# A fused two-layer encoder on one core: the order of the opening stage (warm-up, first loads, scaling of x)

## The chip, the cores and the metric

The kernel runs on one core of one Trainium2 chip. The metric is the time on the device in microseconds (us), from start to end of one execution. Each engine of the core (TensorE, VectorE, ScalarE, GpSimd, SyncE) runs its own list of instructions; semaphores tie them together. In the rows, PE is TensorE's matrix product, PEld its weight load, DVE is VectorE, ACT is ScalarE, POOL is GpSimd and SP is SyncE, which here only issues loads.

## What is computed

x has 512 rows of 1024, mem has 256 rows of 1024, all in fp32. Two layers follow each other, an mLSTM layer and a latent-attention layer, each with attention to the memory. Cut to what matters for the opening:

```python
mem_n = rmsnorm(mem, mem_norm)
mk, mv = split_cols(mem_n @ w_kv, [MEM_WIDTH, MEM_WIDTH])   # memory keys and values, 256 x 512 each
mk = rmsnorm(mk.reshape(bsz, nm, MEM_HEADS, MEM_HEAD_DIM), k_gain)
h = rmsnorm(x, norm_g)                                      # first layer
... = split_cols(h @ w_in, [2 * M_WIDTH, M_WIDTH, M_WIDTH, M_WIDTH, M_HEADS, M_HEADS, MEM_WIDTH, MEM_WIDTH])
```

## The kernel before

Every matrix product is done with operands split into a high part and a low part (`split`: ScalarE writes the high part, VectorE the rest), as three products: high with high, low with high (line 157) and high with low (line 162). Weights come in chunks of 128 x 1024 numbers, 512 KB. `load` (lines 137 to 147) makes the high part "wh" (line 130) and the low part "wl" (line 131) of a chunk; there are two buffers of each.

The opening stage goes up to the first products with x, at about 50 us:

- Line 120 and 121: twenty transpositions of the identity on TensorE, which need only the identity.
- Lines 411 to 413: ScalarE's queue issues the loads of the parameter columns pv (first its first 8 columns, then the rest) and of the positions. The first 8 columns scale the memory (line 133 and 134 in `load_memT`). Lines 481 to 483 multiply columns of the rest on VectorE.
- Lines 488 to 496, 533 to 541: SyncE's queue issues everything else, in this order: the transposed memory's first two pieces, each followed by a half of the first weight chunk, more of the memory with chunks 2 to 4, x in four loads with chunk 5 between them, chunks 6 to 8, the memory by rows for its norm, and then, as buffers come free, the weights of the later products.
- `mem_kv` (lines 244 to 282) is a generator: the memory keys are chunks 1 to 4, the values chunks 5 to 8, each chunk being one turn (one yield), with two row tiles of memory as two accumulators "acc". After the fourth chunk the keys are copied out (line 259), squared head by head (line 187, into "tiny" and "junk" buffers), and scaled on GpSimd (lines 263, 264 and 269). After the eighth, the values are copied out and split, and the keys are transposed (line 280) into two PSUM buffers "tp" and split.
- `x_prep` (lines 503 to 530) is a generator too. It sums the squares of x (lines 187 and 511), takes the power on GpSimd (lines 182 and 183), scales the eight half tiles of x (lines 520 and 522) and ends its first turn. Then, for each of eight groups of 128 columns, four transpositions go into a "tp" buffer (line 527) and a `split` makes that group of hT (hTh and hTl, the transposed, normed x). It yields after every second group.
- `mem_norm` (lines 232 to 242) sums squares of the memory's rows on ScalarE (into "tiny" and "junk" buffers) and takes the power on GpSimd.
- At the end: three turns of `mem_kv`, one of `x_prep`, `mem_norm`, and then `weave`, which gives `x_prep` one turn after each turn of `mem_kv` and lets it finish when `mem_kv` has ended.
- After that `mem_proj` begins: its first group has 264 columns (gates and half of a query projection), three chunks of 3, 3 and 2 groups of hT, with four accumulators "acc", which are all that there are. Its second group has 256 columns and needs the same four.

This program order is not yet the order of the engines' lists. A planner goes through the program with estimated times and puts on each engine the instruction that is ready, earlier ones in the program first. Tiles with one name share a number of buffers ("tp" two, "junk" one, "tiny" forty), and a new tile has to wait until a buffer of its name is free. Only the last stage of the kernel has TensorE's order written out by hand.

Of the kernel before, what the change touches and what calls it, by code (L numbers as in the profile page):

```python
# [12 lines left out]
AF = mybir.ActivationFunctionType  # L13
ALU = mybir.AluOpType
AX = mybir.AxisListType

P = 128
S = 512
NT = 4
# [40 lines left out]
def trunk(ctx: ExitStack, tc: tile.TileContext, pv_d, pos_d, x_d, mem_d, memT_d, wmem_d, wg_d, wa_d, woa_d,  # L60
          wkva_d, wql_d, wb_d, wkvb_d, wqup_d, wob_d, out_d):
    nc = tc.nc
    V, A, G, PE = nc.vector, nc.scalar, nc.gpsimd, nc.tensor
# [11 lines left out]
    def nm(s):  # L75
        cnt[0] += 1
        return f"{s}_{cnt[0]}"
# [3 lines left out]
    def st(shape, tag, bufs=1, dt=F32):  # L81
        return POOLS.get(tag, sp).tile(shape, dt, tag=tag, bufs=bufs, name=nm(tag))
# [6 lines left out]
    def tiny(shape, dt=F32):  # L89
        return st(shape, "tiny", 40, dt)  # L90

    def s2(shape=(P, 512)):
        return st(list(shape), "s2", NS2)

    def acc(shape=(P, 512)):
        return pp.tile(list(shape), F32, tag="acc", bufs=4, name=nm("acc"))
# [4 lines left out]
    def tps(shape=(P, 512)):  # L101
        return pp.tile(list(shape), F32, tag="tp", bufs=2, name=nm("tp"))
# [14 lines left out]
    warm = cp.tile([P, 1], F32, name="warm")  # L117
    A.activation(warm, one, AF.Exp)
    wps = tps([P, P])
    for _ in range(20):  # L120
        PE.transpose(wps, ident, ident)  # L121

    def col(name, i=0):
        o = _PV[name] + i
        return pv[:, o:o + 1]
# [11 lines left out]
    def load(src, nk, ncol, pieces=1, raw=None):  # L137
        n = nk * ncol
        if raw is None:
            raw = wp.tile([P, 1024], F32, tag="wr", bufs=2, name=nm("wr"))  # L140
            nc.sync.dma_start(raw[:, :n], src)
        hi = wp.tile([P, 1024], F32R, tag="wh", bufs=2, name=nm("wh"))
        lo = wp.tile([P, 1024], F32R, tag="wl", bufs=2, name=nm("wl"))
        for i in range(pieces):
            ps_ = slice(i * n // pieces, (i + 1) * n // pieces)
            split(hi[:, ps_], lo[:, ps_], raw[:, ps_])
        return (hi[:, :n].rearrange("p (k c) -> p k c", k=nk), lo[:, :n].rearrange("p (k c) -> p k c", k=nk))

    def prod(items, start, stop):

        left = {}
        for it in items:
            left[id(it[0])] = left.get(id(it[0]), 0) + 1
        seen = set()
        for ps, a_, w_, lhs in items:
            for x in a_:
                PE.matmul(ps, x if lhs else w_[0], w_[0] if lhs else x,  # L157
                          start=start and id(ps) not in seen, stop=False)
                seen.add(id(ps))
        for ps, a_, w_, lhs in items:  # L160
            left[id(ps)] -= 1
            PE.matmul(ps, a_[0] if lhs else w_[1], w_[1] if lhs else a_[0], start=False,  # L162
                      stop=stop and left[id(ps)] == 0)

    def prod_tok(pss, act, w, nk, k0, first, last, done=None):

        n = len(pss)
        step = 1 if last else 2
        for t0 in range(0, n, step):
            prod([(pss[t], act(k0 + k, t), w[k] if isinstance(w, list) else sub(w, slice(None), k), True)  # L170
                  for t in range(t0, min(n, t0 + step)) for k in range(nk)], first, last)
            if last and done:
                done(t0, pss[t0])
            if step == 2 or t0 % 2 == 1:
                yield

    def sub(pair, *idx):
        return (pair[0][idx], pair[1][idx])

    def rpow(out, ss, mul, add, n):  # L180
        t = tiny([P, n])
        G.tensor_scalar(t, ss, mul, add, op0=ALU.mult, op1=ALU.add)  # L182
        G.tensor_tensor(out=out, in0=t, in1=mhalf[:, :n], op=ALU.pow)

    def sqsum(src, accum, scale=1.0):
        j = st([P, 512], "junk", 1, BF16)
        A.activation(j[:, :src.shape[-1]], src, AF.Square, scale=scale, accum_out=accum)  # L187
# [20 lines left out]
    def mem_raw():  # L208
        return [st([P, 2, NM], "s2", NS2) for _ in range(4)]
# [34 lines left out]
    def mem_kv(l, mT, mkT, mv, preload=None):  # L244
        for half in range(2):
            pss = [acc(), acc()]
            for c in range(4):
                i = half * 4 + c
                raw = preload[i] if preload else None
                w = raw if isinstance(raw, tuple) else load(wmem_d[l, i], 2, 512, raw=raw)  # L250
                yield from prod_tok(pss, mT, w, 2, 2 * c, c == 0, c == 3)
            if half == 0:
                ss = tiny([P, 2, 4])
                r = tiny([P, 2, 4])
                mks = []
                for t in range(2):
                    mk = s2()
                    mks.append(mk)
                    A.activation(mk, pss[t], AF.Copy)
                    for h in range(4):  # L260
                        sqsum(mk[:, h * P:(h + 1) * P], ss[:, t, h:h + 1])
                for t in range(2):
                    G.tensor_scalar(ss[:, t], ss[:, t], 1.0 / P, vs_mem[:, t:t + 1], op0=ALU.mult, op1=ALU.add)
                G.tensor_tensor(out=r.rearrange("p a b -> p (a b)"), in0=ss.rearrange("p a b -> p (a b)"),
                                in1=mhalf[:, :8], op=ALU.pow)
                for t in range(2):
                    for h in range(4):
                        hs = slice(h * P, (h + 1) * P)
                        G.tensor_scalar(mks[t][:, hs], mks[t][:, hs], r[:, t, h:h + 1], None, op0=ALU.mult)
            else:  # L270
                for t in range(2):
                    src = pss[t]
                    if preload:
                        src = s2()
                        A.activation(src, pss[t], AF.Copy)
                    split(mv[0][:, t], mv[1][:, t], src, rs_mem[:, t:t + 1])
                for t in range(2):
                    tp = tps([P, 4, P])
                    for h in range(4):
                        PE.transpose(tp[:, h], mks[t][:, h * P:(h + 1) * P], ident)  # L280
                    ts_ = slice(t * P, (t + 1) * P)
                    split(mkT[0][:, :, ts_], mkT[1][:, :, ts_], tp, gg[:, l:l + 1])
# [125 lines left out]
                                    c == 0, c == 5, lambda t, ps: done(half, t, ps))  # L408


    A.dma_start(pv[:, 0:8], pv_d[:, 0:8])
    A.dma_start(pv[:, 8:], pv_d[:, 8:])
    A.dma_start(pos, pos_d)
    tabs = cp.tile([P, 4, NT, 64], F32, name="tabs")
# [66 lines left out]
    V.tensor_tensor(out=gg[:, 0:2], in0=pv[:, _PV["mqg"]:_PV["mqg"] + 2],  # L481
                    in1=pv[:, _PV["mkg"]:_PV["mkg"] + 2], op=ALU.mult)
    V.tensor_tensor(out=gg[:, 2:3], in0=col("qgn"), in1=col("kgn"), op=ALU.mult)
    wraw = st([P, 6, 1024], "yTh"), st([P, 6, 1024], "yTl")
    pre = [wraw[0][:, i] for i in range(6)] + [wraw[1][:, i] for i in range(2)]

    mraw = mem_raw()
    for k in range(2):
        nc.sync.dma_start(mraw[0][:, k], memT_d[:, k])
        nc.sync.dma_start(pre[0][:, k * 512:(k + 1) * 512], wmem_d[0, 0][:, k * 512:(k + 1) * 512])  # L490
    for q in range(1, 4):
        nc.sync.dma_start(mraw[q], memT_d[:, q * 2:q * 2 + 2])
        if q == 1:
# [3 lines left out]
    mT = load_memT(mraw)  # L497
# [6 lines left out]
    def x_prep(xs, hT):  # L504
        rs = tiny([P, NT])
        sa = tiny([P, 2, NT])
        for half in range(2):
            for t in range(NT):
                if t % 2:
                    j = st([P, 512], "m4", 1, BF16)  # L510
                    V.scalar_tensor_tensor(out=j, in0=xs[half][t], scalar=1.0, in1=xs[half][t], op0=ALU.mult,
                                           op1=ALU.mult, accum_out=sa[:, half, t:t + 1])
                else:
                    sqsum(xs[half][t], sa[:, half, t:t + 1])
        V.tensor_tensor(out=sa[:, 0], in0=sa[:, 0], in1=sa[:, 1], op=ALU.add)
        rpow(rs, sa[:, 0], 1.0 / D, EPS, NT)
        for half in range(2):
            for t in range(NT):
                if half and t % 2:
                    A.activation(xs[half][t], xs[half][t], AF.Copy, scale=rs[:, t:t + 1])  # L520
                else:
                    V.tensor_scalar(xs[half][t], xs[half][t], rs[:, t:t + 1], None, op0=ALU.mult)
        yield
        for k in range(KT):
            tp = tps()
            for t in range(NT):
                PE.transpose(tp[:, t * P:(t + 1) * P], xs[k // 4][t][:, (k % 4) * P:(k % 4 + 1) * P], ident)
            split(hT[0][:, k], hT[1][:, k], tp, col("an", k))
            if k % 2:
                yield  # L530
# [5 lines left out]
    xs = load_x(x_d, nc.sync, wraw[1][:, 2:6].rearrange("p a (b c) -> p a b c", b=2), rest)  # L536
# [244 lines left out]
    mT = load_memT()  # L781
# [388 lines left out]
```

## Time and profile before

| | us |
|---|---|
| median of 3 runs | 771.48 |
| lowest and highest | 770.83, 771.83 |
| profiled execution | 771.22 |
| its span, first to last instruction | 769.4 |

The profile is of one execution. In its rows, times are us from the start of the span, and for a row of several instructions the time is from the first one's start to the last one's end. Behind an arrow in brackets stands the idle time of the engine just before the row, and what ended it. Matrix products overlap each other, so a group's time is more than the sum of their starts' distances by the length of the last one.

### The profile page before, as it was taken

Reading aid. Unit: us, or ns where it says so; the run is one execution under the profiler, and the core shown is the slowest. Engines: PE = TensorE matmul, PEld = TensorE weight load, DVE = VectorE, ACT = ScalarE, POOL = GpSimd, SP = SyncE. Lnnn points to the kernel's source line nnn. Section 1 sums busy time; section 2 is a strip of 40 time slices with the busy share of each in tenths; the row PEclk is TensorE's granted clock in tenths of the full one; section 3 lists DMA queues with packets and bytes.
Section 4 is the critical chain, followed back from the end, with each engine's and each line's share of the span. In section 5 each row is a group of like instructions: output and inputs, shape, how many; then the busy total and the mean of one; then the engine's idle time right before and its main releaser. Section 6 shows DMA issues by size and latency. Waiting matters only on the chain.

```text
span 769.4 us, 10978 instructions
## 1 busy us (share of the span) xinstructions
PE 756.1 (98%) x3948; PEld 648.8 (84%) x3948; DVE 486.8 (63%) x985; ACT 409.9 (53%) x958; POOL 133.2 (17%) x259
## 2 busy tenths in 40 slices
PE   9999998999999999999999999999999999999998
PEld 7798887888888888888888878999888888888886
DVE  6743699547778737765434664476778787775422
ACT  6964566345456426546333757367766665644220
POOL 0131010010110101001002131020855351700000
PEclk9999999999999999999999999999999999999999
DMA  9522120322131232225434532221322111511141
GB/s 327 202 89 104 63 79 25 109 90 101 60 107 57 86 106 83 83 83 185 144 137 155 173 110 72 69 67 58 95 75 59 56 59 36 184 55 55 65 155 55
DMA packets 25910, 76.40 MB, mean 99 GB/s; under 512 B 3072, under 2 KB 3968, under 8 KB 25856
## 3 DMA queue, kind: packets, MB, share of 16 engines
q1 hardware_dynamic: 24144, 73.44, 28.7%
q10 hardware_dynamic: 1584, 2.25, 0.8%
q8 instruction: 31, 0.51, 0.3%
q14 instruction: 23, 0.19, 0.1%
q0 software_dynamic: 128, 0.01, 0.0%
HBM read 71.49 MB, written 4.19 MB: 98 GB/s over the span
## 4 chain that ended last, share of the span: by engine, by line
PE 89%; DVE 7%; ACT 2%; POOL 1%; issue 1%; POOLq 0%; DVEq 0%; ACTq 0%
PE acc L157 49%; PE acc L162 24%; PE att L157 3%; PE att L1026 2%; PE att L162 2%; PE tp L1013 1%; PE tp L949 1%; DVE kl L629 1%; DVE tiny L328 1%; DVE wl L131 1%; PE att L715 1%; PE att L716 1%; PE att L714 1%; PE tp L121 1%; PE tp L368 1%
## 5 line engine op out<-in xcount | busy, mean ns | idle before, releaser
L131 DVE TENSOR_TENSOR wl<-wr,wh 128x1024 fp32r<-128x1024 f32 (+5 forms) x117 | 136.8, 1170 | 154.5 <-ACT wh L130 130.0
L130 ACT ACTIVATE wh<-wr 128x1024 fp32r<-128x1024 f32 (+5 forms) x117 | 117.6, 1009 | 134.5 <-PE acc L157 123.3
L157 PE MATMUL acc<-wh,hTl 128*128 128x512 f32 (+3 forms) x320 | 113.3, 366 | 0.0
L157 PE MATMUL acc<-wh,hTh 128*128 128x512 f32 (+3 forms) x320 | 112.4, 368 | 0.3 <-ACT hTh L133 0.3
L157 PE MATMUL acc<-hTh,wh 128*128 128x512 f32 x256 | 101.8, 398 | 0.0
L157 PE MATMUL acc<-hTl,wh 128*128 128x512 f32 x256 | 100.3, 392 | 0.0
L157 PE MATMUL acc<-wh,yTh 128*128 128x512 f32 (+1 forms) x224 | 84.7, 382 | 0.0
L157 PE MATMUL acc<-wh,yTl 128*128 128x512 f32 (+1 forms) x224 | 84.5, 379 | 0.0
L162 PE MATMUL acc<-wl,hTh 128*128 128x512 f32 (+3 forms) x320 | 82.0, 364 | 0.0
L162 PE MATMUL acc<-hTh,wl 128*128 128x512 f32 x256 | 69.6, 391 | 0.0
L157 PEld LDWEIGHTS acc<-wh,hTh 128*128 128x128 f32 x320 | 59.1, 188 | 9.4 <-ACT hTh L133 0.6
L157 PEld LDWEIGHTS acc<-wh,hTl 128*128 128x128 f32 x320 | 59.6, 188 | 8.7 <-DVE hTl L134 0.2
L162 PEld LDWEIGHTS acc<-wl,hTh 128*128 128x128 f32 x320 | 56.5, 188 | 8.6
L162 PE MATMUL acc<-wl,yTh 128*128 128x512 f32 (+1 forms) x224 | 60.1, 378 | 0.0
L157 PEld LDWEIGHTS acc<-hTh,wh 128*128 128x128 f32 x256 | 48.1, 188 | 9.4 <-ACT wh L130 0.3
L162 PEld LDWEIGHTS acc<-hTh,wl 128*128 128x128 f32 x256 | 47.7, 188 | 9.7
L157 PEld LDWEIGHTS acc<-hTl,wh 128*128 128x128 f32 x256 | 48.2, 188 | 9.0
L182 POOL TENSOR_SCALAR tiny<-tiny 128x2 f32<-128x2 f32 (+4 forms) x33 | 8.5, 257 | 236.2 <-ACT junk L187 68.6
L157 PEld LDWEIGHTS acc<-wh,yTh 128*128 128x128 f32 x224 | 42.1, 188 | 7.2
L157 PEld LDWEIGHTS acc<-wh,yTl 128*128 128x128 f32 x224 | 42.1, 188 | 7.1
L162 PEld LDWEIGHTS acc<-wl,yTh 128*128 128x128 f32 x224 | 41.2, 188 | 7.5
L157 PE MATMUL acc<-wh,u 128*128 128x384 f32 (+1 forms) x160 | 38.6, 364 | 1.2 <-ACT u L133 0.7
(285 smaller groups left out, 1418.5 us busy)
## 6 DMA issues: line engine op xcount, KB each, us to landing
wr<-in_wa_dram SPq DMA_DIRECT2D x46, 512.0 KB, 3.2
wr<-in_wb_dram SPq DMA_DIRECT2D x16, 512.0 KB, 3.5
wr<-in_woa_dram SPq DMA_DIRECT2D x12, 512.0 KB, 3.2
wr<-in_wob_dram SPq DMA_DIRECT2D x12, 512.0 KB, 3.2
wr<-in_wmem_dram SPq DMA_DIRECT2D x8, 512.0 KB, 3.5
yTh<-in_wmem_dram SPq DMA_DIRECT2D x5, 512.0 KB, 7.2
yTl<-in_x_dram SPq DMA_DIRECT2D x4, 512.0 KB, 8.7
u<-in_x_dram SPq DMA_DIRECT2D x4, 512.0 KB, 6.1
```

Source lines behind the costliest of these rows:

```text
L121: PE.transpose(wps, ident, ident)
L130: A.activation(hi, src, AF.Copy)
L131: V.tensor_tensor(out=lo, in0=src, in1=hi.bitcast(F32), op=ALU.subtract)
L157: PE.matmul(ps, x if lhs else w_[0], w_[0] if lhs else x, start=start and id(ps) not in seen, stop=False)
L162: PE.matmul(ps, a_[0] if lhs else w_[1], w_[1] if lhs else a_[0], start=False, stop=stop and left[id(ps)] == 0)
L182: G.tensor_scalar(t, ss, mul, add, op0=ALU.mult, op1=ALU.add)
L328: V.tensor_reduce(mx[:, j:j + 1], ps, axis=AX.X, op=ALU.max)
L368: PE.transpose(tp[:, t * P:(t + 1) * P], prs[h][t][:, kt * P:(kt + 1) * P], ident)
L629: V.scalar_tensor_tensor(out=u[:, d:], in0=raw[:, :S - d], scalar=col("cw", (3 - d) * 16 + j), in1=u[:, d:], op0=ALU.mult, op1=ALU.add)
L714: PE.matmul(ps[:, :258], ph[:, blk(c, i)], v[0][:, c], start=c == 0, stop=False)
L715: PE.matmul(ps[:, :258], low(c, i), v[0][:, c], start=False, stop=False)
L1026: PE.matmul(ps[:, i * P:(i + 1) * P], vt[:, c, h * P:(h + 1) * P], pTs[h][:, o:o + P], start=c == 0, stop=c == i)
```

## The change

Four things in the opening stage. Fifteen transpositions of the identity in place of twenty. The first half of the first weight chunk is loaded from ScalarE's queue, between the two loads of pv, and its second half goes ahead of the memory's second piece on SyncE's. The products of the first chunk are ordered so that those with its first half come first, for both row tiles. And x is scaled in two halves, each ahead of the four groups that use it and each ended by a yield, with tiles 1 and 3 of each half on ScalarE and 0 and 2 on VectorE.

```diff
--- before.py
+++ after.py
@@ -117,7 +117,7 @@
     warm = cp.tile([P, 1], F32, name="warm")
     A.activation(warm, one, AF.Exp)
     wps = tps([P, P])
-    for _ in range(20):
+    for _ in range(15):
         PE.transpose(wps, ident, ident)
 
     def col(name, i=0):
@@ -162,13 +162,14 @@
             PE.matmul(ps, a_[0] if lhs else w_[1], w_[1] if lhs else a_[0], start=False,
                       stop=stop and left[id(ps)] == 0)
 
-    def prod_tok(pss, act, w, nk, k0, first, last, done=None):
+    def prod_tok(pss, act, w, nk, k0, first, last, done=None, halves=False):
 
         n = len(pss)
         step = 1 if last else 2
         for t0 in range(0, n, step):
-            prod([(pss[t], act(k0 + k, t), w[k] if isinstance(w, list) else sub(w, slice(None), k), True)
-                  for t in range(t0, min(n, t0 + step)) for k in range(nk)], first, last)
+            its = [(pss[t], act(k0 + k, t), sub(w, slice(None), k), True)
+                   for t in range(t0, min(n, t0 + step)) for k in range(nk)]
+            prod(its[::2] + its[1::2] if halves else its, first, last)
             if last and done:
                 done(t0, pss[t0])
             if step == 2 or t0 % 2 == 1:
@@ -248,7 +249,7 @@
                 i = half * 4 + c
                 raw = preload[i] if preload else None
                 w = raw if isinstance(raw, tuple) else load(wmem_d[l, i], 2, 512, raw=raw)
-                yield from prod_tok(pss, mT, w, 2, 2 * c, c == 0, c == 3)
+                yield from prod_tok(pss, mT, w, 2, 2 * c, c == 0, c == 3, halves=preload is not None and i == 0)
             if half == 0:
                 ss = tiny([P, 2, 4])
                 r = tiny([P, 2, 4])
@@ -408,7 +409,9 @@
                                     c == 0, c == 5, lambda t, ps: done(half, t, ps))
 
 
+    wraw = st([P, 6, 1024], "yTh"), st([P, 6, 1024], "yTl")
     A.dma_start(pv[:, 0:8], pv_d[:, 0:8])
+    A.dma_start(wraw[0][:, 0, 0:512], wmem_d[0, 0][:, 0:512])
     A.dma_start(pv[:, 8:], pv_d[:, 8:])
     A.dma_start(pos, pos_d)
     tabs = cp.tile([P, 4, NT, 64], F32, name="tabs")
@@ -481,13 +484,12 @@
     V.tensor_tensor(out=gg[:, 0:2], in0=pv[:, _PV["mqg"]:_PV["mqg"] + 2],
                     in1=pv[:, _PV["mkg"]:_PV["mkg"] + 2], op=ALU.mult)
     V.tensor_tensor(out=gg[:, 2:3], in0=col("qgn"), in1=col("kgn"), op=ALU.mult)
-    wraw = st([P, 6, 1024], "yTh"), st([P, 6, 1024], "yTl")
     pre = [wraw[0][:, i] for i in range(6)] + [wraw[1][:, i] for i in range(2)]
 
     mraw = mem_raw()
-    for k in range(2):
-        nc.sync.dma_start(mraw[0][:, k], memT_d[:, k])
-        nc.sync.dma_start(pre[0][:, k * 512:(k + 1) * 512], wmem_d[0, 0][:, k * 512:(k + 1) * 512])
+    nc.sync.dma_start(mraw[0][:, 0], memT_d[:, 0])
+    nc.sync.dma_start(pre[0][:, 512:1024], wmem_d[0, 0][:, 512:1024])
+    nc.sync.dma_start(mraw[0][:, 1], memT_d[:, 1])
     for q in range(1, 4):
         nc.sync.dma_start(mraw[q], memT_d[:, q * 2:q * 2 + 2])
         if q == 1:
@@ -514,14 +516,15 @@
                     sqsum(xs[half][t], sa[:, half, t:t + 1])
         V.tensor_tensor(out=sa[:, 0], in0=sa[:, 0], in1=sa[:, 1], op=ALU.add)
         rpow(rs, sa[:, 0], 1.0 / D, EPS, NT)
-        for half in range(2):
-            for t in range(NT):
-                if half and t % 2:
-                    A.activation(xs[half][t], xs[half][t], AF.Copy, scale=rs[:, t:t + 1])
-                else:
-                    V.tensor_scalar(xs[half][t], xs[half][t], rs[:, t:t + 1], None, op0=ALU.mult)
         yield
         for k in range(KT):
+            if k % 4 == 0:
+                for t in range(NT):
+                    if t % 2:
+                        A.activation(xs[k // 4][t], xs[k // 4][t], AF.Copy, scale=rs[:, t:t + 1])
+                    else:
+                        V.tensor_scalar(xs[k // 4][t], xs[k // 4][t], rs[:, t:t + 1], None, op0=ALU.mult)
+                yield
             tp = tps()
             for t in range(NT):
                 PE.transpose(tp[:, t * P:(t + 1) * P], xs[k // 4][t][:, (k % 4) * P:(k % 4 + 1) * P], ident)
```

## Rows read from the trace of the kernel before

**Rows 1.** The page, part 1: busy us, share of the span, instructions, by engine

```profile
PE 756.1 (98%) x3948; PEld 648.8 (84%) x3948; DVE 486.8 (63%) x985; ACT 409.9 (53%) x958; POOL 133.2 (17%) x259
```

**Rows 2.** Stretches: busy us by engine, granted clock, DMA share, GB/s

```profile
5.00:7.25 2.25, 2.25 (x10) 2.06 (x9) 1.48 (x4) 1.10 (x3) 0.00 (x0) 1.00 0.82 252
7.25:20.00 12.75, 12.72 (x54) 9.94 (x54) 10.19 (x19) 10.07 (x20) 0.00 (x0) 1.00 1.04 413
22.18:38.80 16.62, 15.35 (x98) 13.54 (x97) 12.81 (x19) 15.92 (x40) 1.85 (x5) 1.00 0.42 159
```

**Rows 3.** Timeline of TensorE, opening: start, length, line, out<-in, count

```profile
1.81 4.53 PE L121 MATMUL tp<-ident 128*128 128x128 f32 x20 [1.81 <-POOL ident masks.py:199]
5.99 2.99 PE L157 MATMUL acc<-wh,qk 128*128 128x512 f32 x8
...
15.62 1.98 PE L157 MATMUL acc<-wh,qk 128*128 128x512 f32 x8
```

**Rows 4.** Timeline of ScalarE, VectorE and weight loads: first waits for loads

```profile
3.64 0.51 ACT L133 ACTIVATE qk<-s,pv 128x256 fp32r<-128x256 f32 x1 [0.98 <-DMA pv<-in_pv_dram]
...
8.99 1.15 ACT L130 ACTIVATE wh<-yTh 128x512 fp32r<-128x512 f32 x2 [0.48 <-DMA yTh<-in_wmem_dram]
...
9.68 1.69 PEld L157 LDWEIGHTS acc<-wh,qk 128*128 128x128 f32 x8 [0.21 <-ACT wh L130]
...
4.62 0.16 DVE L481 TENSOR_TENSOR gg<-pv 128x2 f32<-128x2 f32 x1 [3.23 <-DMA pv<-in_pv_dram]
```

**Rows 5.** Timeline: the scaling of x, on GpSimd, ScalarE and VectorE

```profile
21.10 1.04 POOL L183 TENSOR_TENSOR tiny<-tiny,mhalf 128x4 f32<-128x4 f32 x1
...
22.18 1.34 ACT L520 ACTIVATE yTl<-yTl,tiny 128x512 f32<-128x512 f32 x2 [0.66 <-POOL tiny L183]
...
22.18 2.46 DVE L522 TENSOR_SCALAR yTl<-yTl,tiny 128x512 f32<-128x512 f32 x6 [1.45 <-POOL tiny L183]
24.56 1.21 DVE L131 TENSOR_TENSOR wl<-yTh,wh 128x1024 fp32r<-128x1024 f32 x1
```

**Rows 6.** Timeline of TensorE in that place

```profile
21.57 2.12 PE L157 MATMUL acc<-wh,qk 128*128 128x512 f32 x8 [0.35 <-ACT wh L130]
23.52 1.04 PE L527 MATMUL tp<-ident,yTl 128*128 128x128 f32 x8
25.83 1.19 PE L162 MATMUL acc<-wl,qk 128*128 128x512 f32 x4 [1.27 <-DVE wl L131]
```

**Rows 7.** Timeline: the memory keys copied out, and squares (u: mem_norm's, s: keys')

```profile
18.09 1.09 ACT L259 ACTIVATE s<-acc 128x512 f32<-128x512 f32 x2 [0.36 <-PE acc L162]
...
25.64 0.63 ACT L187 ACTIVATE junk<-u 128x512 bf16<-128x512 f32 x1
...
30.43 0.45 POOL L239 TENSOR_TENSOR tiny<-tiny 128x2 f32<-128x2 f32 x1 [8.29 <-ACT junk L187]
...
30.83 0.30 ACT L187 ACTIVATE junk<-s 128x128 bf16<-128x128 f32 x1
```

**Rows 8.** Timeline of GpSimd: the memory keys' power and scaling

```profile
39.03 0.27 POOL L263 TENSOR_SCALAR tiny<-tiny,vs_mem 128x4 f32<-128x4 f32 x1 [5.33 <-ACT junk L187]
39.38 1.66 POOL L264 TENSOR_TENSOR tiny<-tiny,mhalf 128x8 f32<-128x8 f32 x1
41.14 5.42 POOL L269 TENSOR_SCALAR s<-s,tiny 128x128 f32<-128x128 f32 x8
```

**Rows 9.** Timeline: the last group of hT, on TensorE, ScalarE and VectorE

```profile
41.34 0.60 PE L527 MATMUL tp<-ident,yTl 128*128 128x128 f32 x4
...
41.97 0.69 ACT L133 ACTIVATE hTh<-tp,pv 128x512 fp32r<-128x512 f32 x1 [0.71 <-PE tp L527]
...
42.70 0.75 DVE L134 SCALAR_TENSOR_TENSOR hTl<-tp,pv,hTh 128x512 fp32r<-128x512 f32 x1 [0.65 <-ACT hTh L133]
```

**Rows 10.** The chain that ended last, 40 to 50: start, length, what

```profile
47.23 0.33 PE tp L280 x3
47.56 0.96 PE acc L157 x8
...
49.00 0.11 PE tp L280
```

## The prediction

> **What bounds the kernel now.** I read the page's first part first: TensorE is busy for 98% of the span [rows 1], so a change can only gain where TensorE waits, and every wait that it adds counts in full. Then the timeline of the first 50 us, engine by engine, for the three places where TensorE waits in the stage that the change touches. The first product starts at 5.99 behind twenty transpositions of the identity that begin at 1.81 [rows 3]. The second chunk's products wait at 9.68 for ScalarE's high part, and ScalarE had itself waited 0.48 us for the load [rows 4]; in the stretch from 7.25 to 20 the DMA engines have no idle share (1.04) [rows 2]. The largest wait is 1.27 us before 25.83, for the low part of the sixth chunk's weights, which stands on VectorE behind six scalings of x [rows 5, 6]. From there to 50 us TensorE does not stop, but what it works on is not independent of the other engines: ScalarE is busy for 15.92 of the 16.62 us from 22.18 to 38.80 [rows 2], and a slow chain through ScalarE and GpSimd (squares of the memory keys, their power, eight scalings) ends at 41.14 + 5.42 = 46.56 [rows 7, 8], just ahead of the last transpositions of line 280 at 47.23 [rows 10].
>
> **Warm-up, first weight half, first chunk by halves.** The twenty transpositions take 4.53 us, 0.23 each [rows 3]; five fewer let TensorE go 1.1 us sooner, at about 5.2. ScalarE's first split starts at 3.64 [rows 4], so the first half's high part can be there by then, and with the chunk taken by halves only that half is needed. But the second chunk cannot start before its own load, which is behind the same bytes as before: its wait at 9.68 stays, and what the first chunk gains is spent there. Gain 0.0. If loads come sooner, the gain is at most the idle share of the DMA engines in the stretch that precedes it, (1 - 0.82) x 2.25 = 0.4 us [rows 2]; I take 0, the nearest rows being those of the full stretch. (The Trainium skill has a rule that speaks against the second queue, "DMA: Bandwidth & Descriptors", section "Issuing engines are not separate DMA queues": loads issued from several engines run on the same 16 DMA engines, and only issue time is saved. By it the 0.4 would be 0; no row of this trace separates the two.) On SyncE's queue one load less is issued, and the weight's second half goes ahead of the second memory piece; the bytes ahead of the second chunk's load are the same. The moved load stands ahead of pv's tail on ScalarE's queue, so that tail lands later, and VectorE's first product (4.62, waiting for it) [rows 4] holds back the low parts queued behind it. One more 256 KB ahead of it at 252 GB/s [rows 2] is 1.0 us; the first chunk's low parts are then late by at most that, still ahead of 9.68, and cost 0 as long as the second chunk's load covers it (1.0 without that cover). The pace of the products: eight take 2.99 us from 5.99 and 1.98 from 15.62 [rows 3]. The granted clock reads 1.00 in all these stretches, so it is the durations that show TensorE at the lower of its two levels (1.2 GHz) through the warm-up and into the first products, and at the higher (2.4 GHz) afterwards. Whether fifteen leave it low for longer is a rival below.
>
> **The scaling in two halves.** Before, VectorE does six scalings in 2.46 us (0.41 each) and ScalarE two in 1.34 (0.67 each), all from 22.18 on, after GpSimd's power [rows 5]; the low part that TensorE waits for starts at 24.56 and takes 1.21 [rows 5]. After, the first half is two on each engine: VectorE is free at 23.0, the low part is done at 24.2, and ScalarE's second tile at 23.52. TensorE ends the chunk's high products at about 23.5, does the eight transpositions (0.88 on its queue, 23.52 to about 24.4 [rows 6]) and finds the low part ready. So the low products start at 24.43 instead of 25.83: a gain of 1.40 us at that place. If the planner puts the low products first, the gain is 0.8. The price is on ScalarE: four scalings instead of two, 1.34 us more, in a stretch with 16.62 - 15.92 = 0.70 us free [rows 2]. What ScalarE does after 22.18 ends 0.64 us later.
>
> **What the added pause does to the order.** This is the part that decides. The scaling now takes two turns of x_prep's loop, each ended by a yield. mem_kv has five turns left when the weave begins. Before, x_prep's four turns (two of the eight transposition groups each) fitted into them. After, the five are: scale, groups 0 and 1, groups 2 and 3, scale, groups 4 and 5. Then mem_kv ends with its last block, which takes two "tp" buffers in PSUM for the memory keys (line 280), and only then come groups 6 and 7. There are two "tp" buffers in all. If the planner hands out the buffers of one name in the program's order, groups 6 and 7 must wait until line 280 has taken its two and given them back, and line 280 waits for GpSimd. The trace speaks for that: the memory keys were in SBUF at 18.09 + 1.09 = 19.18, ScalarE stood idle for 0.66 us before 22.18 [rows 5], and yet their squares, which are early in the program, start at 30.83, right after GpSimd's sum at 30.43 took the small buffer of mem_norm, whose own squares begin at 25.64 [rows 7]; both use the names "tiny" and "junk", mem_norm's first. Nothing else that they need was missing.
>
> Worked out with the times of before: line 280's last input is ready at 46.56 [rows 8]; its transposition and ScalarE's start take 0.30, so 46.86. A split of one 128x512 group goes from ScalarE's start at 41.97 to VectorE's end at 42.70 + 0.75 = 43.45, 1.48 us, and its four transpositions take 0.60 before it [rows 9]. So the buffer is free at 48.34, group 7 is transposed at 48.97 and split at 50.45. The gate product's last chunk needs groups 6 and 7; its last four products, 0.12 each, end at 50.93. The next group of products can't start sooner, since all four accumulators are held by this one. Before, that next group started at 47.56, with one transposition of line 280 (0.11) still to come [rows 10]. The loss is 50.93 - 47.56 - 0.11 = 3.3 us, and the gain of 1.40 is gone, since TensorE now waits for the GpSimd chain and not for its own queue. With ScalarE's 0.64 ahead of the squares it is **3.9 us**.
>
> Bounds: the eight squares were spread over 39.03 - 30.83 = 8.2 us, though one takes 0.30 [rows 7, 8]; back to back they would end 5.8 us sooner, and the chain would cost nothing. Upwards: TensorE will stand for some 3 us, longer than any wait in these rows (1.27 [rows 6], with its pace whole after it). If it falls back to its lower level, the price is bounded by what the start paid: eight products 1.01 slower, twenty transpositions at 0.23 against 0.13 [rows 3, 6], 3.0 together. I take 0 of this, the nearest row being the 1.27.
>
> **Sum.** -0 (opening) -1.40 +1.40 (given back) +3.3 +0.64 = +3.9. The profiled execution took 771.22 us (span 769.4 and 1.8 around it), 0.26 below the median of 771.48; a profiled run after would be at 775.2 with a span of 773.3, the median at 775.4.
>
> **Rivals.** (1) *It does what the half scaling is good for:* groups 6 and 7 are not held behind line 280, or line 280 is done by the time that TensorE gets to the gate's last chunk. Then the 1.40 stays, 770.1, with the loads sooner 769.7, with ScalarE's 0.64 given back 770.7. It decides the matter if group 7 is split by about 43.45 - 1.4 = 42.1. For it: the longest wait is removed for certain. Against it: 46.56. Chance 0.17. (2) *The squares close up:* the order holds but ScalarE, with less to do for TensorE while that waits, does them 2.4 to 5.4 us sooner: 770.0 to 773.0, middle 771.5. Against it: ScalarE's full stretch. Chance 0.10. (3) *The clock:* order not held, but with fifteen transpositions the first two chunks (24 products) run at the lower level. At 0.25 each and 0.23/0.13 = 1.77 times as long that is 4.6 us, less 0.9 of earlier start, 0.2 at the second chunk and 0.35 at 21.57 [rows 6], less 1.40: 773.2. Chance 0.05, since TensorE is busy without a pause in both cases.
>
> **How the numbers follow.** The forecast has 0.68, with a range of its own from 773.1 to 778.4 (from where rival 2 ends, to 3.9 + 3.0 above the median). About 0.2% (1.54 us) is what a measurement here can tell from no change: faster means below 769.94, slower above 773.02. Rival 1 gives 0.10 to faster (with the loads) and 0.07 to same, rival 2 0.10 to same, rival 3 0.02 to same and 0.03 to slower: faster 0.10, same 0.19, slower 0.71. The range from 770.4 to 778.4 holds the forecast, rivals 2 and 3 nearly whole and a part of 1.
>
> **What would show it.** Right: all eight transpositions of line 280 ahead of the last eight of line 527; TensorE idle for 2 to 4 us between 43 and 51, released by ScalarE's or VectorE's parts of hT; the next group at 50 to 52; no wait of 1.27 near 25; the second chunk still at about 9.7. Wrong: group 7 split before 44, or the second chunk's load landing well ahead of 9, which would carry the opening's gain to the end.

## The result, and the profile after

| | before | after |
|---|---|---|
| median, us | 771.40 (4 runs) | 778.65 (4 runs) |
| lowest and highest | 770.83, 771.83 | 778.17, 780.09 |
| profiled execution, its span | 771.22, 769.4 | 778.54, 776.8 |
| ratio to before, 95% interval | | 1.0094 [1.0082, 1.0106] |

The ratios here and below are estimated from all runs of both kernels and can differ a little from the quotient of the medians.

The change makes the kernel 7.2 us slower. The forecast was 775.4 with a range to 778.4: the sign and the place are right, the size is nearly twice the forecast. The traces show that it is lost before 55 us (table "All runs together"). By the page's first part TensorE has the same share of its span as in [rows 1], but five instructions fewer and 5.0 us more busy time, which already points to instructions that took longer:

```profile
PE 761.1 (98%) x3943; PEld 650.4 (84%) x3943; DVE 486.3 (63%) x983; ACT 410.7 (53%) x960; POOL 134.2 (17%) x259
```

The timeline of TensorE in the opening (start, length, line, count) answers to [rows 3] and [rows 6]:

```profile
1.81 3.46 PE L121 MATMUL tp<-ident 128*128 128x128 f32 x15 [1.81 <-POOL ident masks.py:199]
5.93 3.96 PE L157 MATMUL acc<-wh,qk 128*128 128x512 f32 x8 [0.66 <-ACT wh L130]
...
11.03 1.98 PE L157 MATMUL acc<-wh,qk 128*128 128x512 f32 x8
...
22.07 2.11 PE L157 MATMUL acc<-wh,qk 128*128 128x512 f32 x8
24.01 1.03 PE L530 MATMUL tp<-ident,yTl 128*128 128x128 f32 x8
25.00 1.21 PE L162 MATMUL acc<-wl,qk 128*128 128x512 f32 x4
```

The warm-up is 1.07 shorter, and yet the first product starts at 5.93 (5.99 before), now waiting for ScalarE's high part. The wait of 1.27 at the sixth chunk is gone, as it should be: its low products start at 25.00 instead of 25.83. So far the change is ahead. (In between it was behind: the second chunk starts at 11.03, before at about 9.7 [rows 4].) Then the timeline of TensorE from 42 to 55:

```profile
42.92 0.33 PE L281 MATMUL tp<-ident,s 128*128 128x128 f32 x1 [0.47 <-POOL s L270]
44.54 0.36 PE L281 MATMUL tp<-ident,s 128*128 128x128 f32 x1 [1.29 <-POOL s L270]
45.12 2.21 PE L281 MATMUL tp<-ident,s 128*128 128x128 f32 x4 [0.22 <-POOL s L270]
47.74 1.11 PE L530 MATMUL tp<-ident,yTl 128*128 128x128 f32 x4 [0.41 <-DVE v L134]
48.65 0.64 PE L281 MATMUL tp<-ident,s 128*128 128x128 f32 x2
49.63 1.25 PE L157 MATMUL acc<-wh,hTh 128*128 128x264 f32 x4 [0.35 <-ACT hTh L133]
50.68 1.02 PE L530 MATMUL tp<-ident,yTl 128*128 128x128 f32 x4
51.38 0.80 PE L157 MATMUL acc<-wh,hTl 128*128 128x264 f32 x4
52.48 0.75 PE L157 MATMUL acc<-wh,hTh 128*128 128x264 f32 x4 [0.29 <-ACT hTh L133]
...
54.97 0.36 PE L157 MATMUL acc<-wh,hTh 128*128 128x256 f32 x1
```

Group 6 of x (line 530) is transposed behind six of the memory keys' eight transpositions (line 281), group 7 behind all eight, and the next group of products (128x256) starts at 54.97. Before, it started 7.66 sooner (the same view of the kernel before):

```profile
47.31 0.36 PE L157 MATMUL acc<-wh,hTh 128*128 128x256 f32 x1
```

In the chain's view the two starts are 55.22 and 47.56 [rows 10], as far apart. The chain of waits in after over the same time (start, length, what) names each link:

```profile
40.48 1.66 POOL tiny L265
...
42.25 3.40 POOL s L270 x4
...
45.70 0.49 PE tp L281
...
46.21 0.70 ACT mkT L133
...
46.93 0.76 DVE v L134
...
47.74 1.13 PE tp L530 x4
...
48.89 0.70 ACT hTh L133
...
49.63 1.25 PE acc L157 x4
50.88 0.83 PE tp L530 x4
...
51.73 0.70 ACT hTh L133
...
52.48 0.75 PE acc L157 x4
```

Before, this chain was TensorE's alone from 40 to 50 [rows 10]. Now it runs through GpSimd, then ScalarE and VectorE (who free a "tp" buffer at 47.69), then group 6, and only then group 7. In the table by stretches (busy us with count for TensorE, weight loads, VectorE, ScalarE, GpSimd; then the granted clock), TensorE's wait and the fall of its clock are seen together:

```profile
42.00:45.00 3.00, 1.13 (x6) 0.51 (x4) 1.25 (x1) 0.82 (x1) 2.89 (x4) 0.95 0.00 0
45.00:48.00 3.00, 2.17 (x5) 1.00 (x6) 0.75 (x1) 0.69 (x1) 2.96 (x6) 0.50 0.53 180
48.00:52.00 4.00, 3.65 (x18) 3.21 (x17) 1.41 (x2) 1.53 (x3) 0.00 (x0) 0.56 0.00 0
```

TensorE is busy for 1.13 of 3.00 us, and then the granted clock is at its lower level (0.50, 1.2 GHz) from about 45 until near 52. There four products of 128x264 take 1.25 us; at the higher level they take 0.64 to 0.65.

### The profile page after: what moved, and what is told of

The parts are those of the page before. It is cut to its first block, busy times and chain, and to the rows that moved or that the text cites. A ratio compares the mean times of both kernels' runs of the same rounds, so it can differ in the third digit from the quotient of the medians.

```text
span 776.8 us, 10967 instructions
## 1 busy us (share of the span) xinstructions
PE 761.1 (98%) x3943; PEld 650.4 (84%) x3943; DVE 486.3 (63%) x983; ACT 410.7 (53%) x960; POOL 134.2 (17%) x259
## 4 chain that ended last, share of the span: by engine, by line
PE 84%; DVE 7%; ACT 3%; DMA 2%; POOL 2%; issue 1%; ACTq 0%; DVEq 0%; POOLq 0%
PE acc L157 46%; PE acc L162 23%; PE att L157 3%; PE att L1029 2%; PE att L162 2%; DMA yTl<-in_x_dram 1%; PE tp L1016 1%; PE tp L952 1%; ACT junk L188 1%; DVE kl L632 1%; DVE wl L131 1%; DVE tiny L329 1%; DMA yTh<-in_wmem_dram 1%; PE att L718 1%; PE att L719 1%
```

## The experiments

Theory: the second scaling's pause puts groups 6 and 7 behind line 281 in the program, the planner gives the two "tp" buffers out in that order, and so TensorE waits for GpSimd's chain. Rivals: the opening's changes (warm-up, loads, first chunk by halves) cost it; or ScalarE's two extra scalings do; or the clock does.

**The pause away (e1_one_pause).** The kernel after, in which only the first scaling ends its turn:

```diff
-                yield
+                if k == 0:
+                    yield
```

> The changed kernel with one edit: the second scaling of x no longer ends its turn, so groups 4 and 5 follow in the same turn and groups 6 and 7 still fit in ahead of the memory keys' transpositions. Theory of the order (the whole loss is that groups 6 and 7 queue for the PSUM buffers behind the keys' transpositions): the stall between 42 and 53 us goes, time 769.5 to 771.5 us. Rival, ScalarE's two additional scalings and the halves themselves: 775 or more stays. Rival, the later rise of TensorE's clock in the opening (at about 10.5 us after the start instead of 7.9): 772.5 to 774 stays.

771.07 against 771.51: 0.9993 [0.9985, 1.0002]. One line takes all of the 7.2 us away, with the rest of the change still in, ScalarE's two extra scalings among it, so those are not the cause. The next group starts at 46.59, ahead of before.

**The pauses alone (e2_pauses_alone).** The kernel before, with nothing but the pauses:

```diff
         for k in range(KT):
+            if k % 4 == 0:
+                yield
             tp = tps()
```

> The kernel before with nothing but two pauses (yields) added in x_prep's loop, ahead of groups 0 and 4, where the change has them; no load, warm-up, scaling or product is touched. Theory of the order: groups 6 and 7 fall behind the keys' transpositions, time 776 to 779 us. If the loss were in the scalings, the loads or the warm-up: 771.4 as before, within 1.

775.76: 1.0052 [1.0036, 1.0067], 4.25 more than the 771.51 of its own comparison. The order is that of after, with the scaling, loads and warm-up of before. The chain:

```profile
41.73 4.54 POOL s L269 x6
...
46.32 0.33 PE tp L280
46.65 0.45 PE tp L529 x4
...
47.12 0.69 ACT hTh L133
...
48.65 0.67 PE tp L529 x4
...
49.35 0.70 ACT hTh L133
```

So the pause is necessary and, by itself, enough for most of the loss, though not for all. One link differs from after. The first "tp" buffer is free at 45.98 here (VectorE's timeline):

```profile
45.23 0.75 DVE L134 SCALAR_TENSOR_TENSOR v<-tp,gg,mkT 128x512 fp32r<-128x512 f32 x1
```

Group 6 still starts only at 46.49, since in TensorE's list it stands behind the sixth of the keys' transpositions, which waits for its scaling until 46.32. The other differences are in the lengths: transpositions and products are at the higher level throughout, and GpSimd's scalings begin at 41.73 instead of 42.25.

**Other buffers, the same order of the program (e3_other_buffers).** All of the change, pause included, but groups 6 and 7 take their PSUM from another name:

```diff
-            tp = tps()
+            tp = tps() if k < 6 else att()
```

> The changed kernel, with both pauses, but groups 6 and 7 are transposed into the two PSUM buffers of another name, which nothing uses at that time. Program order is that of the change. Theory that the buffers' name makes the queue: groups 6 and 7 go ahead of the keys' transpositions again, 769.5 to 771.5 us. Rival, the place in the program alone makes them late (rank, not buffers): 777 or more.

770.28 against the same 771.51: 0.9984 [0.9975, 0.9993]. It is the shared name that holds the groups back, and not their place in the program. TensorE works through, and the keys' transpositions slip in ones and twos between products (chain of waits):

```profile
45.59 0.49 PE acc L157 x4
...
46.32 0.22 PE tp L281 x2
46.54 0.95 PE acc L157 x8
...
48.10 0.11 PE tp L281
```

This version beats both kernels, by 0.16% against before. With twenty warm-up transpositions (**e9_other_buffers_warm20**, the count in line 120 alone) the count makes no difference that these runs can tell:

> The kernel after with twenty transpositions at the start, and the last two groups of hT in buffers of the name acc for attention instead of tp, as in the run before with those buffers (770.28 with fifteen). Theory (the count of the transpositions costs and brings nothing, since the second chunk's load sets the end of the opening): 770.0 to 770.6. Rival (with fifteen the start is earlier by some of the 1.1 us): 770.8 to 771.4. Rival (twenty keep the granted clock's level up sooner, and that brings something in the first chunk): below 770.

770.48 against 771.39: 0.9994 [0.9984, 1.0003], the interval overlapping that of fifteen. The gain over before is small enough for one of the two to reach 1.

**The opening's parts (e4, e5, e6, e8).** Four kernels that differ in them: e1 with twenty warm-ups, before with fifteen, before with the new loads and the first chunk by halves, after with twenty.

> As the one-pause kernel, with twenty warm-up transpositions instead of fifteen. If the opening is covered by the second and sixth chunks' loads (the prediction's step): equal to the one-pause kernel within 0.5 us. Rival, fifteen let TensorE's clock rise 2.8 us later, and that comes through: 1 to 1.5 us faster than the one-pause kernel.

> The kernel before with fifteen warm-up transpositions instead of twenty, nothing else. The prediction's step (covered by the second chunk's load): within 0.5 us of before, 771.0 to 772.0. Rival, the clock rises later and that reaches the end: 772.5 to 774. Rival, the earlier start counts: 770.4 or less.

> The kernel before with the first weight half on ScalarE's queue, the changed load order on SyncE's and the first chunk's products by halves; twenty warm-up transpositions and the old scaling. The prediction's step: within 0.5 us of before, 771.0 to 772.0. Rival, two queues fill the loads' slow start: 0.4 us or more faster. Rival, pv's tail comes later and holds VectorE's low parts back: 0.5 to 1 us slower.

> The changed kernel with twenty warm-up transpositions. If the warm-up has no part in the loss: 778.2 to 779.0. If the late rise of the clock in the opening (10.6 us against 7.9) is a part of it: 776 to 777.6.

| | median, us | ratio to before |
|---|---|---|
| e1 with 20 (e4) | 771.00 | 0.9992 [0.9983, 1.0001] |
| before with 15 (e5) | 771.38 | 1.0002 [0.9993, 1.0011] |
| before with the new loads and halves (e6) | 771.55 | 1.0001 [0.9993, 1.0010] |
| after with 20 (e8) | 778.37 | 1.0089 [1.0075, 1.0103] |

None of them moves the time. That clears the opening: the rise of the clock was later with fifteen in the profile of after, but twenty in the same kernel cost the same 7 us. One thing did go wrong in the opening: with the moved load, VectorE's first product, which waits for pv's tail, starts at 6.77 in e6 and 6.79 in after (4.62 in [rows 4]), and in e6 TensorE waits 0.78 us in its first chunk for a part that VectorE writes. That wait is covered later.

**The clock (e7_filled_gap).** The kernel after, with products that nobody reads behind each of the eight keys' transpositions, to keep TensorE busy (two products are four instructions):

```diff
                     for h in range(4):
                         PE.transpose(tp[:, h], mks[t][:, h * P:(h + 1) * P], ident)
+                        for _ in range(2):
+                            PE.matmul(fill[:, h], mks[t][:, h * P:(h + 1) * P], mks[t][:, h * P:(h + 1) * P],
+                                      start=True, stop=True)
```

> The changed kernel with two unused 128x128 products behind each of the eight transpositions of the memory keys, so that TensorE has something to do while it waits for GpSimd; the results are not read, and the order of the other instructions of TensorE is that of the change. If a part of the loss is the fall of TensorE's clock in that wait (granted clock 0.50 from 44.7 to 51.5): the clock stays at 1.00 and the time falls by 0.7 to 2.5 us, to 776.2 to 778.0. If the clock costs nothing there, since TensorE waits anyway: 778.6 or more.

777.56: 1.0079 [1.0063, 1.0094]. The clock stays up, in the stretches where it had been at 0.50 and 0.56:

```profile
45.00:48.00 3.00, 3.00 (x28) 2.85 (x27) 0.75 (x1) 0.84 (x2) 2.53 (x5) 1.00 0.41 158
48.00:52.00 4.00, 3.66 (x28) 3.07 (x27) 2.17 (x3) 1.89 (x3) 0.00 (x0) 1.00 0.00 0
```

More work on TensorE, and 1.1 us less time in the medians. In the traces it is 1.7 (the next group starts at 53.30), but 0.44 of that is an earlier begin of GpSimd's scalings (41.81), ahead of the first added product. The intervals of the two ratios overlap, so the 1.1 is an estimate. It is more likely too low than too high, since some of the added instructions stand on the chain (0.45 us for each four). The fall of the clock is a part of the loss, and the smaller one.

**A shorter chain (e10_keys_on_vector).** The kernel after, with the keys' eight scalings on VectorE:

```diff
-                        G.tensor_scalar(mks[t][:, hs], mks[t][:, hs], r[:, t, h:h + 1], None, op0=ALU.mult)
+                        V.tensor_scalar(mks[t][:, hs], mks[t][:, hs], r[:, t, h:h + 1], None, op0=ALU.mult)
```

> The kernel after, with the eight scalings of the memory keys (line 270) on VectorE in place of GpSimd. The order of the buffers stays as in the kernel after: the last two groups of hT still stand behind line 281. Theory (the stall is the length of the chain that line 281 waits for): GpSimd's power ends at 42.13 in the kernel after and its eight scalings at 47.96, 5.7 us later; on VectorE a 128x512 scaling takes 0.41, so eight of 128x128 should take 1 to 1.5 us. The eight transpositions of line 281 are then done by about 44 to 45, the next group of products starts 3 to 4 us sooner than at 54.97, and the time is 774 to 776 instead of 778.65; with the fall of the granted clock gone, another 1.1 less, 773 to 775. Rival (it is the order alone, whatever the length of the chain, for instance since the splits of ScalarE and VectorE one after another fill the same time): 777.5 to 779. Rival (VectorE has no room here, so its eight scalings delay the low parts of the weights): 776 or more, with new waits for line 131 after 42.

775.19: 1.0049 [1.0035, 1.0063]. With the order untouched, a chain that is shorter gives back 3.5 us of the 7.2. Its chain of waits shows what is late next:

```profile
42.51 1.34 DVE s L270 x7
43.85 1.13 DVE wl L131
44.98 0.67 DVE v L134
...
45.70 1.97 PE tp L530 x8
47.67 2.45 PE acc L157 x13
```

The scalings end at 43.85 instead of 47.96, but a low part of weights and the keys' own splits stand between them and the "tp" buffer, on VectorE; group 6 starts at 45.70 instead of 47.74, groups 6 and 7 follow each other at once, and the next group starts at 51.42. The granted clock falls here too (0.62 from 45 to 48), but for less long (0.86 from 48 to 52, against 0.56 in after), so a part of the 3.5 us may be the clock's.

**Beside GpSimd (e11_vector_beside_gpsimd).** One of GpSimd's eight scalings took 1.64 us in after, the others 0.60. The kernel after, with four scalings of a constant and two products of two SBUF inputs on VectorE from the power on, unread:

```diff
+                    fl = att([P, 4, P])
+                    tf = ident.unsqueeze(1).broadcast_to([P, 4, P])
+                    for _ in range(4):
+                        V.tensor_scalar(fl, tf, r[:, 0, 0:1], None, op0=ALU.mult)
+                    for _ in range(2):
+                        V.tensor_tensor(out=fl, in0=tf, in1=tf, op=ALU.mult)
```

> The kernel after with six more operations on VectorE as soon as the memory keys' power is there, so that they run beside the eight scalings of GpSimd: four scalings of a constant 128x512 (one input from SBUF) and then two products of two 128x512 inputs, both from SBUF. Their results go to a spare PSUM tile and are read by nobody. It is for what stretched one of GpSimd's scalings (1.64 us in place of 0.60 beside the low part of line 131, which reads 128x1024 twice from SBUF). If an operation of VectorE with two inputs in SBUF holds GpSimd's one back: 0.60 or so for GpSimd's scalings beside the four scalings on VectorE, and one or two of over 0.9 beside the two products and beside line 131, which now comes later. If anything that VectorE does in SBUF holds it back: longer ones beside the four scalings too. If it has nothing to do with VectorE and belongs to the second scaling: the second is long, whatever VectorE does then. The time is of no interest: 778 to 781.

It took 778.23. Its timelines of VectorE, and of GpSimd's third and fourth scaling:

```profile
41.85 0.75 DVE L271 TENSOR_SCALAR att<-ident,tiny 128x512 f32<-128x512 f32 x1 [2.09 <-POOL tiny L265]
42.52 1.25 DVE L131 TENSOR_TENSOR wl<-wr,wh 128x1024 fp32r<-128x1024 f32 x1
43.70 2.32 DVE L271 TENSOR_SCALAR att<-ident,tiny 128x512 f32<-128x512 f32 x3
...
44.14 1.18 POOL L277 TENSOR_SCALAR s<-s,tiny 128x128 f32<-128x128 f32 x2
```

Beside the four scalings of VectorE the GpSimd's take their 0.59 each; the long one (42.52, 1.64) is again the one that starts with line 131. The two products were put so late (47.13) that they met only the rest of the last scaling, so they decide nothing.

**All runs together.** Where the next group of products starts in each profile, and how long that execution took:

| | next group starts, us | execution, us | difference |
|---|---|---|---|
| before | 47.31 | 771.22 | 723.91 |
| e5, e6 | 47.54, 47.58 | 771.40, 771.53 | 723.86, 723.95 |
| e9, e3, e4, e1 | 45.80, 46.30, 46.35, 46.59 | 770.12, 770.69, 770.79, 771.07 | 724.32, 724.39, 724.44, 724.48 |
| e10 | 51.42 | 774.76 | 723.34 |
| e2 | 52.58 | 776.09 | 723.51 |
| e7 | 53.30 | 776.84 | 723.54 |
| e11, e8 | 54.59, 54.89 | 778.23, 778.41 | 723.64, 723.52 |
| after | 54.97 | 778.54 | 723.57 |

What follows takes 723.3 to 724.5 us, whatever came before. The stage decides, and nothing is given back or lost later, but for some 0.5 us in e1, e3, e4 and e9: there three to six transpositions of line 281 (0.11 each) are still to come behind that start, in before, e5 and e6 one, and in the others none.

## Why the prediction was wrong in size

**The opening, 0.0: right as a size; the cover was only in part the one named.** e5 and e6 are within 0.02% of before. In e5 the second chunk waits for its weights and starts at 9.74, as forecast. But it starts at 10.16 in e6 and at 11.03 in after, and VectorE's first product, which waits for pv's tail, starts at 6.00 (e4) to 6.79 (after) in the kernels with the moved load, 1.4 to 2.2 us later than the 4.62 of [rows 4] and not 1.0 at most. What covers this is the sixth chunk. Before it, ScalarE waits for a load of x (ScalarE's timeline of before, then of after):

```profile
15.39 0.63 ACT L187 ACTIVATE junk<-yTl 128x512 bf16<-128x512 f32 x1 [0.61 <-DMA yTl<-in_x_dram]
15.89 0.63 ACT L188 ACTIVATE junk<-yTl 128x512 bf16<-128x512 f32 x1 [0.62 <-DMA yTl<-in_x_dram]
```

In twelve of the thirteen profiles the sixth chunk's products start 6.17 to 6.19 us behind the end of that wait (6.34 in e7), whatever the opening did.

**The sixth chunk, -1.40 and given back: right as a mechanism, too high as a size.** The wait of 1.27 is gone in all runs with the halves. But the chunk's high products start at 22.11 in e1 and 22.38 in e3 (21.57 in [rows 6]), in e3 waiting for ScalarE's part of the weights, so that at the low products 0.8 and 0.3 are left, and e1 gained 0.4 in all. The later start varies with the execution and not with the change: ScalarE's wait for x ends later both with the new loads (15.92 in e1, 16.21 in e3, but 15.32 in e7) and with the old ones (15.95 in e2). Counted from the chunk's start, the low products come 1.07 to 1.36 sooner than before in the runs with the halves. Why less of that reaches the end is not shown.

**The order, +3.3: right in cause, wrong in its working.** e1, e2 and e3 show the cause. The terms, with the forecast's 0.64 of ScalarE in the first:

| link | forecast | measured in after | miss |
|---|---|---|---|
| GpSimd's scalings begin | 41.78 | 42.25 | +0.47 |
| from there to a free "tp" buffer | 7.20 | 5.44 | -1.76 |
| from there to group 7's split | 2.11 | 5.51 | +3.40 |
| from there to the last product's end | 0.48 | 1.80 | +1.32 |

They add up to 3.43; the median missed by 3.25. (The last product ends at 55.00 in the chain's view, by which the forecast counts; two transpositions of line 319, 0.22 together, stand between it and the next group there.) The first term's miss is the later load of x (15.89 against 15.39); ScalarE's 0.64 was about right: from the end of that wait to the scalings it is 25.75 in before and 26.36 in after. The second is not like for like, since the forecast's 7.20 goes to the last of the two buffers and the measured 5.44 to the first, and that it makes the sum's miss smaller is luck.

The step that failed is the third. I let groups 6 and 7 go side by side, a buffer for each, with one round behind the last buffer ("the buffer is free at 48.34, group 7 is transposed at 48.97 and split at 50.45"). The runs show one after the other. The first buffer is free after four of the eight scalings (3.40 us), and then a whole round of transposition, ScalarE and VectorE passes for group 6 is over before group 7 begins at 50.68. VectorE's timeline shows which buffer that was:

```profile
49.61 0.75 DVE L134 SCALAR_TENSOR_TENSOR hTl<-tp,pv,hTh 128x512 fp32r<-128x512 f32 x1 [1.93 <-ACT hTh L133]
50.28 0.74 DVE L134 SCALAR_TENSOR_TENSOR v<-tp,gg,mkT 128x512 fp32r<-128x512 f32 x1
52.45 0.75 DVE L134 SCALAR_TENSOR_TENSOR hTl<-tp,pv,hTh 128x512 fp32r<-128x512 f32 x1 [1.44 <-ACT hTh L133]
```

Group 7 begins after group 6's buffer is free (50.36) and before the keys' second one is (51.02). In e2 and e7 it begins 0.05 and 0.06 behind group 6's (48.65 and 49.38), ahead of the other. So both groups went through the same buffer: I counted one round, and there were two, 5.51 us in place of 2.11. (In e2, at the higher clock, the two take 4.2 us, from 46.65 to 50.82.) In e10, where the two buffers come free at 45.64 and 46.30, the eight transpositions do follow at once. The fourth term is mis-sized for a plain reason: behind the last split there stand not four products but the twelve from 53.26 to 54.97, the low ones and those with the weights' low part, which the order of the list keeps there.

**The clock, bounded at +3.0 and taken as 0: wrong choice.** TensorE's idle time, which I put at some 3 us, is 14.00 - 10.62 = 3.4 us from 42 to 56. Filling it kept the clock up (e7, priced at about 1.1), and twenty warm-ups did not (e8: 0.52 from 45 to 52), so the fall belongs to that stretch and not to the warm-up. It lengthens the third term above. I had chosen by the nearest row, a single wait of 1.27; in after it was several waits in a row with only a few transpositions between them. But how much idle time does it is not shown: in e2, with 14.00 - 11.58 = 2.4 us in the same stretch, the clock stayed up, and in e10, with 14.00 - 12.38 = 1.6, most of it one wait of 1.46, it fell.

**Signs.** Of those named, the wait of 1.27 was gone. TensorE was idle for 8.00 - 5.42 = 2.6 us between 43 and 51, in the range named, but 1.5 of it were waits for GpSimd's scalings and not for parts of hT. Six, not eight, of the keys' transpositions stood ahead of group 6; the next group came at 54.97 and not at 50 to 52, the second chunk at 11.03 and not at about 9.7.

**Rivals.** (1) did not occur with this order, and is what e1 and e3 make of it: 771.07 and 770.28, against the 770.1 worked out. (2) did not: GpSimd's power ended later, not sooner. (3) had no part in the time: the clock did rise later in after's profile and in e1's, but e1, e5 and e8 show no price.

What stays open: of the 7.2 us, 4.25 are the pauses' alone (e2) and about 1.1 the clock's. For the remaining 1.9 no run gives a cause. The traces offer two: the scalings begin 0.5 later than in e2 (42.25 against 41.73, though x had landed at the same time, 15.89 and 15.95), and TensorE's list has another order. The clock's price, too, may be more than 1.1.

## What to carry to other kernels

A yield in a generator is a change of program order, and where tiles of one name are handed out in program order, it decides who waits for whose buffer: count the turns on both sides of a weave before adding one, and give a late user a name of its own. When several users have to pass through few buffers, count how many go through the same one, a whole round for each, and what stands behind the last one in the list. And price an idle TensorE with the work that follows at the lower clock, not with the idle time alone.

## What the runs showed of the hardware that was not expected

- A GpSimd scaling of 128x128 takes 0.60 us, but 1.30 to 1.64 when it starts during VectorE's 1.22 to 1.27 us difference of two 128x1024 inputs in SBUF (line 131). It was the seventh of the eight in before (44.64, beside VectorE's 44.29 to 45.51), the second in after (42.85, beside 42.85 to 44.10), the second and the seventh in e3 (44.24 and 47.84, beside those from 43.80 and 47.54), and in e11 none of those beside VectorE's scalings with one input. So it is neither the place in the row nor any work of VectorE; that the two inputs are the cause is what these cases agree on, and it was not tried by itself. The Trainium skill ("SBUF — State Buffer", section "Who interferes with whom") has it that a VectorE instruction with two SBUF inputs contends with a GpSimd one that reads SBUF, and that one with at most one SBUF input, outside VectorE's two-port modes, does not. These runs agree, with 0.7 to 1.0 us for each meeting.
- The rise of TensorE's clock in the opening differs from execution to execution of like openings: from 5.93 the first eight products take 3.96 us in after, and in e10, with the same opening, the first six take 1.67 from 6.08. The second chunk then starts at 11.03 and 9.50. By the transpositions of x both are at the same place (24.01 and 23.97): both sixth chunks start 6.18 behind the end of ScalarE's wait for x (15.89 and 15.84).
